# Token tiles 0 and 1 go through w_v unnormed, and their norm is applied afterwards

## Chip, cores and metric

The kernel runs on one core of a Trainium2 chip. The metric is the device time of one execution in microseconds. Before the change the median of three runs is 1320.01 us (1317.74 to 1320.96).

The engines are named as in the profile: PE is TensorE (matmuls and transposes), DVE is VectorE, ACT is ScalarE, POOL is GpSimd, SP is SyncE, which here only issues loads. Each has its own queue of instructions, and takes them in order.

## The reference, cut to what matters

The model is one layer: a mixing block (a gated convolution beside attention) and a feed-forward block, 1024 tokens by 1024 channels in 32-bit floats. Only its first step is touched here: the norm of the tokens and the projection to v and the forget logits.

```python
def rmsnorm(x, g):
    return x * lax.rsqrt(jnp.mean(x * x, axis=-1, keepdims=True) + 1e-6) * g

h = rmsnorm(x, norm_mix_pre)          # 1024 tokens x 1024 channels
proj = einsum("bsd,dn->bsn", h, w_in) # columns 1024:1544 are v (512) and 8 forget logits
logf = log_sigmoid(f_logit + b_f)
```

The factor of a token, rs = (mean(x*x) + 1e-6)^-0.5, is one number per row of h. It commutes with the projection: rs * ((x * g) @ w) is the same as (rs * x * g) @ w.

## The kernel before

The 1024 tokens are eight tiles of 128 rows. For each tile the kernel squares x with a sum along the row (ACT, output `ssq`), forms the factor on POOL (`rms_scale`: an addition `va`, then a power `r`), scales x to `hn`, and turns `hn` with eight 128x128 transposes on PE (`tp`) so that channels lie on the partitions. Each 32-bit operand is split in two halves, a high one (ACT copies, rounded) and a low one (DVE subtracts), and a product is the sum of three matmuls: high by high ("hh"), high by low ("hl"), low by high ("lh"). The tile's v and forget logits are `pv`: 8 channel blocks x 3 products x 2 column halves of 260, that is 48 matmuls a tile. `wvh` and `wvl` are the halves of w_v, block by block; `hB11h/hB11l` and `hB21h/hB21l` are the halves of the turned tiles 0 to 3 (channels 0 to 511 and 512 to 1023), and `hraw` is their unsplit copy, which later tiles subtract from. `vs` is pv copied out by ACT; POOL writes it to memory (`v_dram`), and DVE adds the bias `bf` to its last eight columns (`ff`).

Tiles 0 and 1 come while w_v is still being loaded, and are ordered by hand; the statements of that part are kept in program order on every engine (`strict[0] = engines`). Tile 0 is loaded in two halves and squared in two halves. Its factor comes first, then DVE scales one half and ACT the other, and only then do the transposes run (`t0.turn(hn)`). Since the gain g is per channel, it is put on after the transposes, by DVE (`scale`: hraw<-tp,gcol, where `gcol` is g turned by the small transpose `gps`); then ACT takes the high half (`high`) and DVE the low (`low`). Tile 1 goes the same way. In between, PE multiplies what is ready (`Parts.run`), and where nothing is, it multiplies zeros into a spare bank (`spins`, 512 columns each; 16 in all).

From tile 2 on, `norm` scales a whole tile in one DVE operation (hn<-xt,r,gm), two tiles ahead of its products: PE gets tile t+1's transposes, then tile t's 48 matmuls. There are three buffers for x, so the load of tile t+3 is issued only when tile t's buffer is free (`load_x` at the end of `norm_rest`). SP issues loads in the order of the statements.

After the eight tiles (`v_tile`), PE goes on with the products of the q, k and gate columns (`b`), for which the operands of all tiles are used.

Of the kernel before, what the change touches and what calls it, by code (L numbers as in the profile page):

```python
# [10 lines left out]
F32 = mybir.dt.float32  # L11
# [6 lines left out]
P = 128  # L18
# [28 lines left out]
def block_kernel(  # L47
# [114 lines left out]
    nc.vector.memset(ones, 1.0)  # L162
# [50 lines left out]
    av, av_close = pool("av")  # L213
    psa, psa_close = pool("psa", 4, space=PSUM)

    def load_x(st):
# [31 lines left out]
    nc.scalar.activation(warm, ones[:, 0:1], AF.Square)  # L248
    wvh = av.tile([P, KT, VF], F32R, name="wvh")
    wvl = av.tile([P, KT, VF], F32R, name="wvl")  # L250

# [4 lines left out]
        vs_tile()  # L256


    spin = psa.tile([P, 2, NC], F32, tag="pv", name="spin", bufs=2)
    zero = ap.tile([P, 4, P], F32R, tag="b12h", name="zero", bufs=2)  # L260
    nc.vector.memset(f32(zero), 0.0)
    sub(mask, tri, ident)
    nc.vector.tensor_scalar(mask, mask, BIG, None, op0=ALU.mult)

    def spins(n):
        for _ in range(n):
            nc.tensor.matmul(
                spin[:, 0, :], zero[:, 0, :], zero.rearrange("p a b -> p (a b)"),
                start=True, stop=True,
            )  # L270

    spins(7)
    gps = psa.tile([P, 4, P], F32, tag="mm", name="gps")[:, 0, :KT]
    nc.tensor.transpose(gps, g8, ident[:KT, :KT])
    nc.sync.dma_start(gm, norm_mix_pre[0].partition_broadcast(P))
    spins(3)

    def wv_high(k):
        copy(wvh[:, k, :], wrs[k])
# [3 lines left out]

    def norm_sum(st):

        xt = xq.popleft()
        hn = ap.tile([P, D], F32, tag="hn", name="hn", bufs=2)
        ssq = st_tile("ssq")
        nc.scalar.activation(hn, xt, AF.Square, scale=ROOT, accum_out=ssq)
        return xt, hn, ssq  # L290

    def norm_rest(st, xt, hn, rs):

        nc.vector.scalar_tensor_tensor(hn, xt, rs, gm, op0=ALU.mult, op1=ALU.mult)
        if st + 3 < ST:
            xq.append(load_x(st + 3))
# [6 lines left out]
    def turned(hn):  # L303

        tps = []
        for q in range(2):
            tp = psa.tile([P, 4, P], F32, tag="mm", name="tp")
            for k in range(4):
                kt = 4 * q + k
                nc.tensor.transpose(tp[:, k, :], hn[:, kt * P : (kt + 1) * P], ident)  # L310
            tps.append(tp)
        return tps

    hraw = av.tile([P, KT, NC], F32, name="hraw")

    class Scaled:


        def __init__(self, st):
            self.ss = slice(st * P, (st + 1) * P)  # L320
            self.ops = [tuple(t[:, :, self.ss] for t in b) for b in (hB11, hB21)]

        def raw(self, q):
            return hraw[:, 4 * q : 4 * q + 4, self.ss]

        def turn(self, hn):
            self.tps = turned(hn)

        def scale(self, q):
            g = gcol[:, 4 * q : 4 * q + 4].unsqueeze(2).broadcast_to([P, 4, P])  # L330
# [94 lines left out]
    xt = xq.popleft()
    hn = ap.tile([P, D], F32, tag="hn", name="hn", bufs=2)
    s2, part = st_tile("s2", 2), st_tile("nm")
    for n, c in enumerate((n1, n2)):
        nc.scalar.activation(
            hn[:, c], xt[:, c], AF.Square, scale=ROOT, accum_out=s2[:, n : n + 1]  # L430
        )
        if n == 0:
            nc.vector.tensor_scalar(part, s2[:, 0:1], EPS, None, op0=ALU.add)
    rs0 = rms_scale(s2[:, 1:2], part)
    nc.vector.tensor_scalar(hn[:, n1], xt[:, n1], rs0, None, op0=ALU.mult)
    nc.scalar.activation(hn[:, n2], xt[:, n2], AF.Identity, scale=rs0)
    nc.vector.tensor_copy(gcol, gps)
    xq.append(load_x(3))
    t0, t1 = Scaled(0), Scaled(1)
    t0.turn(hn)  # L440
    spins(4)
    xt1, hn1, ssq1 = norm_sum(1)
    wv_high(0)
    t0.scale(0)
    t0.high(0)

    def between():
        t0.scale(1)
        t0.low(0)

    rs1 = rms_scale(ssq1, between=between)
    v0, v1 = Parts(t0.ops), Parts(t1.ops)
    v0.run("hh", 0)
    spins(1)
    wv_high(1)
    v0.run("hh", 1)
    v0.run("lh", 0, 1)
    t0.high(1)
    nc.vector.tensor_scalar(hn1[:, n1], xt1[:, n1], rs1, None, op0=ALU.mult)
    nc.scalar.activation(hn1[:, n2], xt1[:, n2], AF.Identity, scale=rs1)  # L460
    xq.append(load_x(4))
    spins(1)
    t1.turn(hn1)
    wv_low(0)
    wv_high(2)
    v0.run("hh", 2)
    v0.run("lh", 2)
    v0.run("hl", 0)
    wv_high(3)
    t0.low(1)  # L470
    v0.run("hh", 3)
    v0.run("lh", 3)
    wv_high(4)
    t1.scale(0)
    t1.high(0)
    wv_low(1)
    v0.run("hh", 4)
    v0.run("lh", 4)
    v0.run("hl", 1)
    wv_high(5)  # L480
    t1.low(0)
    t1.scale(1)
    v1.run("hh", *range(4))
    v1.run("lh", *range(4))
    wv_high(6)
    wv_low(2)
    t1.high(1)
    v1.run("hl", 0, 1)
    t1.low(1)
    wv_high(7)  # L490
    wv_low(3)
    for k in (2,):
        v0.run("hl", k)
        v1.run("hl", k)
    v0.run("hh", 5)
    v0.run("lh", 5)
    xt2, hn, ssq2 = norm_sum(2)
    v0.run("hl", 3)
    v1.run("hl", 3)
    wv_low(4)  # L500
    v0.run("hh", 6)
    v0.run("lh", 6)
    sum3 = norm_sum(3)

    def between():
        for k in (5, 6, 7):
            wv_low(k)

    rs2 = rms_scale(ssq2, between=between)
    v1.run("hh", 4, 5)  # L510
    v1.run("lh", 4, 5)
    v0.run("hl", 4)
    v1.run("hl", 4)
    norm_rest(2, xt2, hn, rs2)
    v0.run("hh", 7)
    v0.run("lh", 7)
    v1.run("hh", 6)
    v1.run("lh", 6)
    v0.run("hl", 5, 6, 7)
    rs3 = rms_scale(sum3[2])  # L520
    v_out(0, v0.pv)
    v1.run("hh", 7)
    v1.run("lh", 7)
    v1.run("hl", 5, 6)
    cur = turn(2, hn)
# [1793 lines left out]
```

## Time and profile before

| what | before |
|---|---|
| median of three runs | 1320.01 us |
| lowest, highest | 1317.74, 1320.96 us |
| the profiled execution | 1319.89 us |
| its span in the trace | 1318.0 us |
| PE busy | 1308.8 us, 99% of the span |
| DVE, ACT, POOL busy | 917.2, 555.8, 185.6 us |
| PE's share of the chain that ended last | 96% |

The profiled execution is 1.89 us longer than its span. The page's chain of waits goes back from the last instruction to whatever released each step, so its shares say which engine set the end; the timeline views list one engine's instructions in order of start, and "idle before" there is the time the engine stood still ahead of an instruction, with what released it.

### The profile page before, as it was taken

To read this page: it belongs to the slowest core of one execution; us is meant where nothing else is said; L and a number is where in the kernel's file an instruction comes from. 1 tells how busy PE (TensorE), PEld (TensorE's weight loads), DVE (VectorE), ACT (ScalarE), POOL (GpSimd) and SP (SyncE) were. 2 spreads that over 40 slices of the span, in tenths; PEclk is the share of its full clock that TensorE was granted. 3 is DMA by queue.
4 is the path that set the end of the run, shared out by engine and by line. 5 is a ranking of instruction groups with operands and counts; after the bars stand their busy time and mean duration, and the time that the engine had idled before them with its cause. 6 is when DMAs were issued, how large, how long until landed. Compare 5 with 4: busy or idle time off the path is not lost.

```text
span 1318.0 us, 17686 instructions
## 1 busy us (share of the span) xinstructions
PE 1308.8 (99%) x6695; PEld 1089.3 (83%) x6695; DVE 917.2 (70%) x1313; ACT 555.8 (42%) x869; POOL 185.6 (14%) x347
## 2 busy tenths in 40 slices
PE   9999999999999999999999999999999999999998
PEld 8988888888888888888888888888888888888886
DVE  6883768776756866676667788866766666677674
ACT  6631323243355766513678432222322234344451
POOL 3101001012112212011223112111001110000001
PEclk9999999999999999999999999999999999999999
DMA  6352423556536445674476565533323337966551
GB/s 225 90 160 88 141 61 119 183 194 195 196 128 206 154 138 166 210 257 132 131 231 227 174 198 193 176 120 104 99 86 115 110 106 271 364 217 192 159 169 64
DMA packets 168389, 215.71 MB, mean 164 GB/s; under 512 B 11480, under 2 KB 113952, under 8 KB 168304
## 3 DMA queue, kind: packets, MB, share of 16 engines
q1 hardware_dynamic: 146352, 141.40, 34.5%
q0 software_dynamic: 21952, 73.19, 15.3%
q8 instruction: 52, 0.85, 0.3%
q14 instruction: 33, 0.27, 0.1%
HBM read 153.41 MB, written 61.15 MB: 163 GB/s over the span
## 4 chain that ended last, share of the span: by engine, by line
PE 96%; ACT 1%; DVE 1%; DMA 1%; issue 1%; POOL 0%; DVEq 0%; POOLq 0%; SPq 0%; ACTq 0%
PE b L76 61%; PE pd L76 16%; PE pv L76 4%; PE pbb L76 3%; PE pba L76 3%; PE po L76 2%; PE tps L76 2%; PE sp L76 2%; PE tp L76 1%; PE ma L76 1%; PE mb L76 1%; DMA raw<-in_w_gate_up_dram 0%; ACT raw L76 0%; DMA xt<-in_x_dram 0%; DVE x L76 0%
## 5 line engine op out<-in xcount | busy, mean ns | idle before, releaser
L76 DVE TENSOR_TENSOR c<-c,b 128x512 f32<-128x512 f32 x215 | 146.8, 683 | 96.9 <-PE b L76 87.4
L76 DVE TENSOR_TENSOR lo<-raw,hi 128x1024 fp32r<-128x1024 f32 (+1 forms) x91 | 109.7, 1205 | 81.2 <-PE b L76 65.7
L76 ACT ACTIVATE hi<-raw 128x1024 fp32r<-128x1024 f32 (+1 forms) x98 | 99.7, 1017 | 102.0 <-PE b L76 68.5
L76 ACT ACTIVATE hi<-sx 128x1024 fp32r<-128x1024 f32 x44 | 46.8, 1063 | 207.2 <-PE b L76 181.3
L76 DVE TENSOR_TENSOR lo<-sx,hi 128x1024 fp32r<-128x1024 f32 x44 | 53.8, 1223 | 39.6 <-PE b L76 37.9
L76 PE MATMUL b<-w12h,lo 128*128 128x512 f32 x208 | 80.9, 389 | 0.0
L76 PE MATMUL b<-w12h,hi 128*128 128x512 f32 x204 | 79.4, 389 | 0.0
L76 PE MATMUL b<-w12l,hi 128*128 128x512 f32 x204 | 79.4, 389 | 0.0
L76 PE MATMUL b<-hh,hi 128*128 128x512 f32 x176 | 69.0, 392 | 0.0
L76 PE MATMUL b<-hh,lo 128*128 128x512 f32 x176 | 68.5, 389 | 0.0
L76 PE MATMUL b<-hl,hi 128*128 128x512 f32 x176 | 68.5, 389 | 0.0
L76 DVE TENSOR_TENSOR sx<-raw 128x512 f32<-128x512 f32 x78 | 53.6, 687 | 20.0 <-DMA raw<-in_w_in_dram 10.3
L76 PE MATMUL b<-w,s4h 128*128 128x512 f32 x208 | 64.0, 389 | 0.0
L76 PE MATMUL pd<-hi,lo 128*128 128x512 f32 x160 | 62.3, 389 | 0.0
L76 PE MATMUL pd<-hi 128*128 128x512 f32 x160 | 61.9, 390 | 0.0
L76 PE MATMUL pd<-ghi 128*128 128x512 f32 x148 | 57.6, 389 | 0.0
L76 PE MATMUL pd<-ghi,glo 128*128 128x512 f32 x148 | 57.6, 389 | 0.0
L76 PE MATMUL pd<-glo,ghi 128*128 128x512 f32 x148 | 57.6, 389 | 0.0
L76 POOL DMA_DIRECT2D a_dramA<-um x33 | 17.9, 541 | 276.6 <-DVE um L76 275.8
L76 PE MATMUL b<-hT34h,hi 128*128 128x512 f32 x136 | 53.0, 390 | 0.4 <-DVE c L76 0.4
L76 PE MATMUL b<-hT34h,lo 128*128 128x512 f32 x136 | 52.9, 389 | 0.0
L76 PE MATMUL b<-hT12h,hi 128*128 128x512 f32 x136 | 52.9, 389 | 0.0
(451 smaller groups left out, 3572.8 us busy)
## 6 DMA issues: line engine op xcount, KB each, us to landing
raw<-in_w_gate_up_dram SPq DMA_DIRECT2D x52, 512.0 KB, 3.8
raw<-in_w_in_dram SPq DMA_DIRECT2D x35, 512.0 KB, 3.8
a_dramS<-um POOLq DMA_DIRECT2D x44, 256.0 KB, 3.1
a_dramA<-um POOLq DMA_DIRECT2D x33, 256.0 KB, 2.6
sg<-sg_dram SPq DMA_DIRECT2D x32, 256.0 KB, 4.2
graw<-a_dramS SPq DMA_DIRECT2D x14, 512.0 KB, 4.3
sg_dram<-c POOLq DMA_DIRECT2D x24, 256.0 KB, 2.5
raw<-in_w_down_dram SPq DMA_DIRECT2D x11, 512.0 KB, 4.4
```

What stands on the lines that cost most here:

```text
L76: ins = getattr(self.engine, name)(*args, **kw)
```

## The change

Tiles 0 and 1 are no longer scaled by their factor ahead of the transposes. PE turns x itself, half a tile at a time, and the products with w_v are those of x times g. The factor is put on at three later places: on v's rows, by the ACT copy out of pv (`v_out(..., scale=...rs)`); and on the columns of `hraw` that belong to tiles 0 and 1, by POOL, after a matmul of ones with the two factors on a diagonal (`rp`) has spread them over the partitions; `settle` then splits these columns anew into hB11 and hB21, where later products read them. Both tiles are loaded in halves, the first block of w_v between tile 0's halves. The squares of tiles 0 and 1 are whole tiles, in place in the x buffer; tile 1's now comes after those of tiles 2 and 3. The third x load, the row of gains `gm` and the fourth x load are issued later than before relative to w_v's blocks. The 32-byte bias row `bf`, broadcast to all partitions, is issued by POOL after tile 0's factor. The small load of gains for `gps` moves to ACT's queue. There are 4 spins of 512 columns and 10 of 256 in place of 16 of 512.

```diff
-        for c in (n1, n2) if st == 0 else (slice(0, D),):
+        for c in (n1, n2) if between else (slice(0, D),):
             nc.sync.dma_start(xt[:, c], rows[:, c])
+            if between and c is n1:
+                between()
...
-    xq = deque([load_x(0)])
-    nc.sync.dma_start(g8, norm_mix_pre[0].rearrange("(k p) -> k p", p=P))
-    xq.append(load_x(1))
-    for k in range(8):
+    nc.scalar.dma_start(g8, norm_mix_pre[0].rearrange("(k p) -> k p", p=P))
+    xts = [load_x(0, load_wv), load_x(1, lambda: None)]
+    for k in range(7):
         load_wv()
-        if k == 4:
-            xq.append(load_x(2))
+    xq = {2: load_x(2)}
...
+        def square(self):
+            self.ssq = st_tile("ssq")
+            nc.scalar.activation(
+                self.xt, self.xt, AF.Square, scale=ROOT, accum_out=self.ssq
+            )
...
+        nc.scalar.activation(
+            vs.rearrange("p (n c) -> p n c", n=2), pv[:, :, :hv], AF.Copy, **kw
+        )
...
+    def square(t):
+        if t < 2:
+            firsts[t].square()
+        else:
+            later[t] = norm_sum(t)
+        if t == 0:
+            nc.sync.dma_start(gm, norm_mix_pre[0].partition_broadcast(P))
+            xq[3] = load_x(3)
+        if t == 1:
+            xq[4] = load_x(4)
...
+    steps_(
+        "wh0 s00 wl0 x01 z1 h00 sq0 l00 phh00 phl00 z1 x10 s01 plh00 z1 pw0 x11 z2 s10 h01 wh1 l01 h10 "
...
+    hn = norm_rest(2, *later[2][:2], norms[2])
+    steps_("plh06 pw3 phh16 plh16 phl05 phl15 phh07")
+    hn3 = norm_rest(3, *later[3][:2], norms[3])
+    steps_("pw1")
+    cur = turn(2, hn)
+    hn = hn3
+    steps_("plh07 phl06 phl07")
+    v_out(0, parts[0].pv, scale=firsts[0].rs)
+    steps_("phh17 plh17 phl16 phl17")
+    v_out(1, parts[1].pv, scale=firsts[1].rs)
...
+    for t, f in enumerate(firsts):
+        nc.gpsimd.tensor_scalar(dg[:, t, :], ident, f.rs, None, op0=ALU.mult)
+    rp = psa.tile([P, 4, P], F32, tag="mm", name="rp")[:, :2, :]
+    nc.tensor.matmul(flat_(rp), ones, flat_(dg), start=True, stop=True)
+    copy(rb, flat_(rp))
...
+    for q in range(2):
+        nc.gpsimd.tensor_tensor(
+            raw_both(q), raw_both(q), rb.unsqueeze(1).broadcast_to([P, 4, 2 * P]),
+            op=ALU.mult,
         )
...
+        for q, (hh, hl) in enumerate((hB11, hB21)):
+            split(hh[:, :, both], hl[:, :, both], raw_both(q))
...
             v_out(2, v2.pv)
+            settle()
```

The order of the instructions on PE, at the start of the program, before (`spin` are the zeros, `tp` the transposes):

```order
L76 MATMUL spin<-zero 128x512 x7
L76 MATMUL gps<-ident,gm 128x8
L76 MATMUL spin<-zero 128x512 x3
L76 MATMUL tp<-ident,hn 128x128 x8
L76 MATMUL spin<-zero 128x512 x4
L76 MATMUL pv<-wvh,hB11h 128x260 x2
L76 MATMUL spin<-zero 128x512
L76 MATMUL pv<-wvh,hB11h 128x260 x2
L76 MATMUL pv<-wvh,hB11l 128x260 x4
L76 MATMUL spin<-zero 128x512
L76 MATMUL tp<-ident,hn 128x128 x8
```

And now:

```order
L76 MATMUL spin<-zero 128x512 x4
L76 MATMUL tp<-ident,xt 128x128 x4
L76 MATMUL gps<-ident,gm 128x8
L76 MATMUL spin<-zero 128x256 x4
L76 MATMUL tp<-ident,xt 128x128 x4
L76 MATMUL spin<-zero 128x256
L76 MATMUL pv<-wvh,hB11h 128x260 x2
L76 MATMUL pv<-wvl,hB11h 128x260 x2
L76 MATMUL spin<-zero 128x256
L76 MATMUL tp<-ident,xt 128x128 x4
L76 MATMUL pv<-wvh,hB11l 128x260 x2
L76 MATMUL spin<-zero 128x256
```

The transposes of tile 0 read `xt` in place of `hn`, come in fours, and follow 4 spins where they followed 10.

On PE, later, where tile 2's products begin and tile 3's transposes follow, before:

```order
L76 MATMUL pv<-wvh,hB11h 128x260 x8
L76 MATMUL pv<-wvl,hB11h 128x260 x8
L76 MATMUL pv<-wvh,hB11l 128x260 x6
L76 MATMUL tp<-ident,hn 128x128 x8
L76 MATMUL pv<-wvh,hB11l 128x260 x2
```

And now:

```order
L76 MATMUL pv<-wvh,hB11h 128x260 x8
L76 MATMUL pv<-wvl,hB11h 128x260 x8
L76 MATMUL pv<-wvh,hB11l 128x260 x6
L76 MATMUL rp<-rs,ones 128x256
L76 MATMUL tp<-ident,hn 128x128 x8
L76 MATMUL pv<-wvh,hB11l 128x260 x2
```

The matmul with ones stands between 22 of tile 2's products and tile 3's transposes.

On POOL, from tile 1's factor on (`v_dram` the write of v, `rs<-ident` the diagonals, `hraw<-hraw,rs` the multiplication of the columns), one piece of the difference:

```order
-L76 TENSOR_SCALAR va<-ssq 128x1
-L76 TENSOR_TENSOR r_481<-va,power 128x1
-L76 TENSOR_SCALAR va<-ssq 128x1
-L76 TENSOR_TENSOR r_562<-va,power 128x1
+L76 TENSOR_SCALAR rs<-ident,r_277 128x128
+L76 TENSOR_SCALAR rs<-ident,r_412 128x128
+L76 TENSOR_TENSOR hraw<-hraw,rs 128x4x256 x2
+L76 TENSOR_SCALAR va<-ssq 128x1
+L76 TENSOR_TENSOR r_564<-va,power 128x1
 L76 DMA v_dram<-vs 128x512
```

Between the factor of tile 4 (which now stands ahead of the second write of v) and that of tile 5 there are now two diagonals and two multiplications. On ACT the square of tile 5 stands behind the two copies that read their results (`hB11h<-hraw` and `hB21h<-hraw`, 128x4x256), and the square of tile 4 stands ahead of tile 1's `vs`:

```order
L76 ACTIVATE vs<-pv,r_277 128x520
L76 ACTIVATE hn,ssq<-xt 128x1024
L76 ACTIVATE vs<-pv,r_412 128x520
L76 ACTIVATE rs<-rp 128x256
L76 ACTIVATE hraw<-tp 128x4x128 x2
L76 ACTIVATE hB11h<-tp 128x4x128
L76 ACTIVATE hB21h<-tp 128x4x128
L76 ACTIVATE hB11h<-hraw 128x4x256
L76 ACTIVATE hB21h<-hraw 128x4x256
L76 ACTIVATE hn,ssq<-xt 128x1024
```

## Rows read from the trace of the kernel before

**Rows 1.** Page: busy time by engine, and the chain's shares.

```profile
PE 1308.8 (99%) x6695; PEld 1089.3 (83%) x6695; DVE 917.2 (70%) x1313; ACT 555.8 (42%) x869; POOL 185.6 (14%) x347
...
PE 96%; ACT 1%; DVE 1%; DMA 1%; issue 1%; POOL 0%; DVEq 0%; POOLq 0%; SPq 0%; ACTq 0%
```

**Rows 2.** Chain of waits, first 30 us: start us, us, engine, operation.

```profile
1.17 3.29 DMA xt<-in_x_dram
...
6.82 1.97 PE tp L76 x8
8.79 1.71 PE spin L76 x4
10.50 0.43 PE pv L76 x2
...
12.17 0.87 PE tp L76 x8
13.04 10.31 PE pv L76 x86
...
24.48 2.91 PE pv L76 x22
```

**Rows 3.** Chain of waits from 24 to 64 us: tile 5's transposes.

```profile
38.01 0.87 PE tp L76 x8
```

**Rows 4.** Two stretches: us, busy us by engine, PEclk, DMA share, GB/s.

```profile
5.00:10.00 5.00, 4.90 (x16) 3.77 (x17) 2.43 (x5) 3.85 (x9) 1.64 (x4) 1.00 0.95 338
25.00:60.00 35.00, 35.00 (x298) 35.00 (x298) 31.18 (x46) 23.59 (x39) 6.12 (x13) 1.00 0.28 88
```

**Rows 5.** Timeline of ACT: start us, us, engine, line, operation, out<-in.

```profile
24.80 0.61 ACT L76 ACTIVATE vs<-pv 128x520 f32<-128x520 f32 x1
...
25.76 1.09 ACT L76 ACTIVATE hn<-xt 128x1024 f32<-128x1024 f32 x1
26.71 0.22 ACT L76 ACTIVATION_READ_ACCUMULATOR hn<-xt 128x1 f32 x1
```

**Rows 6.** Timeline of DVE, same columns.

```profile
8.83 0.69 DVE L76 TENSOR_TENSOR hraw<-tp,gcol 128x512 f32<-128x512 f32 x1 [0.16 <-PE tp L76]
9.44 0.68 DVE L76 TENSOR_TENSOR hB11l<-hraw,hB11h 128x512 fp32r<-128x512 f32 x1
...
19.69 1.28 DVE L76 SCALAR_TENSOR_TENSOR hn<-xt,r,gm 128x1024 f32<-128x1024 f32 x1
...
65.29 1.22 DVE L76 TENSOR_TENSOR lo<-raw,hi 128x1024 fp32r<-128x1024 f32 x1 [0.78 <-ACT hi L76]
```

**Rows 7.** Timeline of POOL, same columns.

```profile
18.10 0.87 POOL L76 TENSOR_TENSOR r<-va,power 128x1 f32<-128x1 f32 x1
...
25.71 0.54 POOL L76 DMA_DIRECT2D v_dram<-vs  x1 [1.01 <-ACT vs L76]
27.02 0.22 POOL L76 TENSOR_SCALAR va<-ssq 128x1 f32<-128x1 f32 x1 [0.77 <-DVE hn L76]
27.33 0.57 POOL L76 TENSOR_TENSOR r<-va,power 128x1 f32<-128x1 f32 x1
```

**Rows 8.** POOL, groups by shape: count, busy us, mean ns, idle before.

```profile
L76 POOL TENSOR_TENSOR rows<-rows,mask 128x128 f32<-128x128 f32 x32 | 14.5, 457 | 62.2 <-DVE nm L76 56.3 <-DMA rows<-c_dram 5.8
```

**Rows 9.** Timeline around 441 us: a POOL row, the DVE row beside it.

```profile
440.82 0.90 POOL L76 TENSOR_TENSOR yb<-cb,mask 128x128 f32<-128x128 f32 x1
...
440.62 1.65 DVE L76 TENSOR_TENSOR yl<-raw,yh 128x512 fp32r<-128x512 f32 x2
```

**Rows 10.** DMA issues, 20.9 to 25 us: count, KB, us to landing.

```profile
xt<-in_x_dram SPq DMA_DIRECT2D x1, 512.0 KB, 3.5
```

**Rows 11.** The same for the first 30 us.

```profile
xt<-in_x_dram SPq DMA_DIRECT2D x7, 512.0 KB, 4.3
```

**Rows 12.** PE, the plain 32-bit matmuls with ones: min/median/max ns.

```profile
L76 PE MATMUL cps<-s,ones x2: 275/275/275, 134.4 to 134.5; 128*128 128x64 f32 x2
```

**Rows 13.** Timeline of PE: the first matmul with the next weights' low half.

```profile
69.82 0.39 PE L76 MATMUL b<-hB11h,lo 128*128 128x512 f32 x1
```

More of the change, by code (lines that the diff above doesn't have):

```diff
@@ L214, in block_kernel, with load_x @@
     psa, psa_close = pool("psa", 4, space=PSUM)
-    def load_x(st):
+    def load_x(st, between=None):
         xt = ax.tile([P, D], F32, tag="x", name="xt", bufs=3)
         rows = x2d[st * P : (st + 1) * P, :]
-        for c in (n1, n2) if st == 0 else (slice(0, D),):
+        for c in (n1, n2) if between else (slice(0, D),):
             nc.sync.dma_start(xt[:, c], rows[:, c])
+            if between and c is n1:
+                between()
         return xt
@@ L237, in block_kernel @@
     strict[0] = engines
+    zero = ap.tile([P, 4, P], F32R, tag="b12h", name="zero", bufs=2)
+    nc.vector.memset(f32(zero), 0.0)
+    nc.vector.memset(ones, 1.0)
     gm = ax.tile([P, D], F32, name="gm")
     g8 = gm[:KT, :P]
-    xq = deque([load_x(0)])
-    nc.sync.dma_start(g8, norm_mix_pre[0].rearrange("(k p) -> k p", p=P))
-    xq.append(load_x(1))
-    for k in range(8):
+    nc.scalar.dma_start(g8, norm_mix_pre[0].rearrange("(k p) -> k p", p=P))
+    xts = [load_x(0, load_wv), load_x(1, lambda: None)]
+    for k in range(7):
         load_wv()
-        if k == 4:
-            xq.append(load_x(2))
+    xq = {2: load_x(2)}
     warm = st_tile("warm")
-    nc.scalar.activation(warm, ones[:, 0:1], AF.Square)
+    nc.scalar.activation(warm, f32(zero)[:, 0, 0:1], AF.Square)
     wvh = av.tile([P, KT, VF], F32R, name="wvh")
@@ L256, in block_kernel, with flat_, spins @@
         vs_tile()
-    spin = psa.tile([P, 2, NC], F32, tag="pv", name="spin", bufs=2)
-    zero = ap.tile([P, 4, P], F32R, tag="b12h", name="zero", bufs=2)
-    nc.vector.memset(f32(zero), 0.0)
+    def flat_(t):
+        return t.rearrange("p a b -> p (a b)")
+    spin = psa.tile([P, 4, P], F32, tag="mm", name="spin")
+    spin = flat_(spin)
     sub(mask, tri, ident)
     nc.vector.tensor_scalar(mask, mask, BIG, None, op0=ALU.mult)
-    def spins(n):
+    def spins(n, w=4):
         for _ in range(n):
             nc.tensor.matmul(
-                spin[:, 0, :], zero[:, 0, :], zero.rearrange("p a b -> p (a b)"),
+                spin[:, : w * P], zero[:, 0, :], flat_(zero[:, :w, :]),
                 start=True, stop=True,
             )
-    spins(7)
+    spins(4)
     gps = psa.tile([P, 4, P], F32, tag="mm", name="gps")[:, 0, :KT]
-    nc.tensor.transpose(gps, g8, ident[:KT, :KT])
-    nc.sync.dma_start(gm, norm_mix_pre[0].partition_broadcast(P))
-    spins(3)
     def wv_high(k):
@@ L301, in norm, with turned @@
         return norm_rest(st, xt, hn, rms_scale(ssq))
[L303 to L312, printed above, removed]
+    def turned(hn, q):
+        tp = psa.tile([P, 4, P], F32, tag="mm", name="tp")
+        for k in range(4):
+            kt = 4 * q + k
+            nc.tensor.transpose(tp[:, k, :], hn[:, kt * P : (kt + 1) * P], ident)
+        return tp
     hraw = av.tile([P, KT, NC], F32, name="hraw")
-    class Scaled:
+    class First:
         def __init__(self, st):
@@ L321, in __init__, with turn @@
             self.ops = [tuple(t[:, :, self.ss] for t in b) for b in (hB11, hB21)]
+            self.tps, self.xt = {}, xts[st]
         def raw(self, q):
             return hraw[:, 4 * q : 4 * q + 4, self.ss]
-        def turn(self, hn):
-            self.tps = turned(hn)
+        def turn(self, q):
+            self.tps[q] = turned(self.xt, q)
         def scale(self, q):
@@ L337, in low, with root @@
             sub(self.ops[q][1], self.raw(q), f32(self.ops[q][0]))
+        def square(self):
[3 more added lines that the diff above has]
+            )
+        def root(self):
+            self.rs = rms_scale(self.ssq)
     def turn(st, hn):
         ss = slice(st % 4 * P, (st % 4 + 1) * P)
-        tps = turned(hn)
+        tps = [turned(hn, q) for q in range(2)]
         if st < 4:
@@ L412, in block_kernel, with v_out @@
     flast = []
-    def v_out(st, pv):
+    def v_out(st, pv, **kw):
         vs = vs_tile()
-        copy(vs.rearrange("p (n c) -> p n c", n=2), pv[:, :, :hv])
+        nc.scalar.activation(
+            vs.rearrange("p (n c) -> p n c", n=2), pv[:, :, :hv], AF.Copy, **kw
+        )
         nc.gpsimd.dma_start(v_dram[st * P : (st + 1) * P, :], vs[:, :AW])
@@ L422, in v_out @@
             flast.clear()
[L425 to L430, printed above, removed]
-        )
[L432 to L525, printed above, removed]
@@ L526, in block_kernel, with root @@
-    v1.run("hl", 7)
+    firsts = [First(t) for t in range(2)]
+    later, norms = {}, {}
+    def square(t):
[8 more added lines that the diff above has]
+            xq[4] = load_x(4)
+    def root(t):
+        if t < 2:
+            firsts[t].root()
+            if t == 0:
+                nc.gpsimd.dma_start(bf, b_f[0].partition_broadcast(P))
+        else:
+            norms[t] = rms_scale(later[t][2])
@@ new lines, in step, with steps_ @@
+    def step(o):
+        n = int(o[-1])
+        if o[0] == "z":
+            return spins(n, 2)
+        if o[:2] in ("wh", "wl", "sq", "pw"):
+            return dict(wh=wv_high, wl=wv_low, sq=square, pw=root)[o[:2]](n)
+        if o[0] == "x":
+            return firsts[int(o[1])].turn(n)
+        if o[0] == "p":
+            return parts[int(o[3])].run(o[1:3], n)
+        getattr(firsts[int(o[1])], dict(s="scale", h="high", l="low")[o[0]])(n)
+    def steps_(row):
+        for o in row.split():
+            step(o)
@@ new lines, in block_kernel @@
+    firsts[0].turn(0)
+    nc.tensor.transpose(gps, g8, ident[:KT, :KT])
+    spins(4, 2)
+    nc.vector.tensor_copy(gcol, gps)
+    parts = [Parts(f.ops) for f in firsts]
+    steps_(
[5 rows of a table added]
+    )
+    hn = norm_rest(2, *later[2][:2], norms[2])
[7 more added lines that the diff above has]
+    steps_("phh17 plh17 phl16 phl17")
@@ new lines, in block_kernel, with raw_both @@
+    v_out(1, parts[1].pv, scale=firsts[1].rs)
+    z = z_tile("rs")
+    dg = z[:, : 2 * P].rearrange("p (t c) -> p t c", t=2)
+    rb = z[:, 2 * P : 4 * P]
+    for t, f in enumerate(firsts):
[3 more added lines that the diff above has]
+    copy(rb, flat_(rp))
+    both = slice(0, 2 * P)
+    def raw_both(q):
+        return hraw[:, 4 * q : 4 * q + 4, both]
```

11 lines of the change are left out of this document (4 added, 7 removed), and 4 rows, old and new, of the table parts.

## The prediction, made before the changed kernel ran

> **What bounds the kernel now.** First the page: PE is busy 99% of the span and makes 96% of the chain that ended last [rows 1]. So the end moves only by what moves PE's work, and the place to look is the one stretch that the change touches, the first 60 us. The chain of waits there [rows 2] leaves the loads and the norm of tile 0 at 6.82 us, when PE starts tile 0's transposes, and from then on stays on PE, whatever the other engines do. What counts is therefore where tile 2's first product stands (24.48 us before) and whether PE then keeps going: the products of tiles 2 to 7 that follow are the same in both kernels.
>
> In these first microseconds PE runs at two speeds. Eight transposes take 1.97 us from 6.82 on and 0.87 us from 12.17 on; two matmuls of pv take 0.43 us at 10.50, and 86 of them 10.31 us later, 0.120 each [rows 2]. So the first rows run at 1.2 GHz and the later at 2.4, and the step lies at about 10.9 us, after PE had been busy, mostly with spins, for some 9 us. The granted clock reads 1.00 for that stretch [rows 4], so it is the rows that tell the level, not that column.
>
> **What the early start is worth.** Before, PE does, ahead of 10.9 us, eight transposes and two products of pv that count, the rest is spins. From there at full speed: tile 1's eight transposes 0.87, 94 products at 0.120 = 11.28, tile 2's transposes 0.87, two spins of 0.23 = 0.46: 13.5, which gives 24.4 against 24.48 in the row.
>
> Now the transposes read x itself. The factor of tile 0, between the landing of its second half at 1.17 + 3.29 = 4.46 and 6.82 [rows 2], is off the path. Against that a block of w_v, 260 KB, is loaded ahead of the second half; at the 338 GB/s of that stretch [rows 4] it costs 0.8 to 1.2 us, so the second four transposes start at 5.3 to 5.7. From 5.5, in the new order and at half speed (0.215 each): 12 transposes, six products and spins as wide as one product bring PE to 10.4; to 10.9 two or three more products. Ahead of the step stand now 16 transposes and about 8.5 products. Left: 87.5 x 0.120 = 10.5, two short spins 0.23, tile 2's transposes 0.87: tile 2 starts at 10.9 + 11.6 = 22.5. **Gain 1.95 us.** Bounds: if x lands 1.2 late, some five instructions (0.55 us) less; if the clock steps up 2.4 us sooner, as PE's work starts no later than before, half of that more, 1.2. If gaps in PE's new start delay the step, less by half the delay.
>
> **The wait that takes its place.** In front of tile 3's transposes PE now meets `rp`, the matmul that spreads the factors. It waits for POOL's two diagonals, and POOL takes its queue in order: tile 4's `va` and `r`, tile 1's write of v, then the diagonals. So `rp` waits for tile 4's square, that for tile 4's load, and that for the buffer which tile 2's scaling on DVE gives back. Priced row by row: the scaling started at 19.69 and takes 1.28 [rows 6]. DVE's queue ahead of it loses two half-tile scalings and holds as before 16 operations 0.61 apart (8.83, 9.44); I let it move with PE, by 1.95, so that it ends at 19.0. The one load that ran alone took 3.5 us [rows 10]: 22.5. The square with its read takes 1.17 [rows 5]: 23.7. `va` and `r` together, 27.02 to 27.90 [rows 7]: 24.6. The write's issue, 0.54 [rows 7]: 25.1. The diagonals, 128x128 with one operand, are not in the trace; they lie between 0.22 (one column [rows 7]) and 0.46 (two operands [rows 8]), I take 0.33 each: 25.8 to 25.9.
>
> PE comes to `rp` at 22.5 + 2.9 [rows 2] = 25.4. **Wait 0.5**, and 0.3 more for the halting of POOL beside DVE that the next paragraph shows: 0.8, bounds 0 and 1.9 (the load at the median of 4.3 [rows 11] and both haltings). `rp` itself, 256 columns of plain 32-bit, has two bounds: 0.12 as 260 columns of pv, and four times the 0.275 of 64 columns [rows 12], 1.1; I take 0.4, nearer the first, since 0.275 is mostly the length of one pass. Then tile 3's second four transposes need a bank that ACT gives back with its copy of `rp`: 256 columns, under the 0.61 of 520 [rows 5], against four transposes of 0.43 that hide it: 0.25 visible, bounds 0 and 0.6.
>
> POOL is held up when DVE reads two operands from SBUF. At 18.10 a power of one column took 0.87 beside DVE's subtractions of weights, at 27.33, beside an operation with one operand in PSUM, 0.57 [rows 7]; the 128x128 mask, 0.457 in the mean of 32 [rows 8], took 0.90 beside DVE's yl<-raw,yh, which itself took 1.65 for two [rows 9] where two of DVE's 512-column steps are 0.61 apart [rows 6]. So both lose some 0.3 to 0.45 us a meeting. The Trainium skill, "SBUF — State Buffer", section "Who interferes with whom" and the points on the two sides ahead of it, says that the second of two such instructions is blocked until the first is through; the rows of 441 us agree in sign, and by that rule a long multiplication of POOL would hold DVE for its whole length.
>
> **The columns of tiles 0 and 1.** POOL multiplies 128x1024 twice. No row has that shape. From one column (0.22) to 128 (0.457) the step is 0.24, and eight of them with the start are 2.15; upper bound eight whole instructions, 3.66; I take 2.2, since the fixed part is paid once. The Trainium skill, "GPSIMD Engine Reference", section 3.1, gives 2.6 cycles an element for tensor_tensor, an estimate of 2.2 us; by it the sum is the same. What is queued behind: ACT's two high copies wait for the results, and behind them stands tile 5's square; on POOL tile 5's factor. After `rp` at 26.2 and its copy: 26.9, multiplications to 29.1 and 31.3, ACT's copy 1.09 [rows 5], tile 5's square 1.17, `va` and `r` 0.9, the scaling 1.28: 35.8. PE needs it for tile 5's transposes, at 38.01 [rows 3] less what is gained, 37.5. It is covered with 1.7 us to spare; the cost is nothing as long as that lasts.
>
> DVE gets two subtractions of 1024, 1.22 each [rows 6], 2.4 in all, between 25 and 60 us, where it is idle 35.0 - 31.2 = 3.8 [rows 4]; what is pushed past that has the slack at the next stage, where the weights' low half is done at 66.5 [rows 6] and first read at 69.82 [rows 13]. No cost. ACT (23.6 of 35 busy) carries the copies and the whole squares. The load of `gps` on ACT's queue, the bias row issued early on POOL and the scale on v's copy are beside other work: nothing.
>
> **Sum.** -1.95 + 0.8 + 0.4 + 0.25 = -0.5 us. On the profiled execution, 1319.89 (span 1318.0 and 1.89 around it), that is **1319.4**; the median of the three runs lies 0.12 above that execution, which I leave aside. A measurement of this kernel tells about 0.3%, 4.0 us, from no change; so this is no change. What makes the estimate stiff: whatever PE gains or loses ahead of 25 us is largely taken up at `rp`, whose time hangs on a load and not on PE.
>
> **Rivals.**
> 1. *The chain to `rp` is quicker.* If DVE's scaling of tile 2 comes 1 us sooner, PE meets no wait there: -1.95 + 0.4 + 0.25 = -1.3, 1318.6; with the earlier step of the clock too -2.5, 1317.4. For it: DVE's queue starts some 3 us earlier. Against: the weights, which it also follows, land at the rate of before [rows 4]. Even with both it is short of 4.0.
> 2. *POOL's multiplication is slow, and PE waits at tile 5's transposes: slower than before.* At 3.66 each the multiplications end at 34.2, and the chain behind them at 38.7, with a halting beside DVE 39.2: PE, due at 37.5, stands 1.2 to 1.7 us. 1319.4 + 1.5 = 1320.9. It decides from about 3.05 each on, where the 1.7 to spare are used. For it: no row of that size, and the haltings [rows 9]. If DVE is held for a whole multiplication, its subtraction for the first settled half is late by up to 2.2, the spare is gone, and the time is the same 1320 to 1321. This is what the rule of the Trainium skill named above would bring here.
> 3. *The load of tile 4 is late.* At 4.3 us in place of 3.5 and with POOL halted twice, `rp` waits 1.9: 1320.5. With rival 2 together 1322.
> 4. *The change doesn't start PE sooner*, because the halves of x are behind the w_v block: the transposes start at 6.7, tile 2 at 23.1. `rp` still comes at 25.9, PE at 26.0: -1.4 + 0.1 + 0.65, the same 1319.3.
>
> **Chances.** The forecast with rival 4, 1318.8 to 1320.2: 0.50. Rival 1: 0.20, of which half for a gain that no row shows and that goes past 4.0 (a start-up at full clock and no wait). Rivals 2 and 3: 0.30, of which 0.09 for sums beyond 4.0. Faster by over 0.3%: 0.10; within 0.3%: 0.81; slower by over 0.3%: 0.09. The range that leaves out a tenth on each side is 1317.0 to 1322.0.
>
> **What would show it.** In the trace of the changed kernel tile 2's first pv<-wvh,hB11h should start at 22.5 (21.3 to 23.2); `rp` should have idle time of PE ahead of it, 0.5 to 1.5 us, released by POOL, and start near 26; POOL's hraw<-hraw,rs should be near 2.2 us, and tile 5's transposes start without idle time. The step of the spacing from 0.215 to 0.120 shows the clock. I am wrong if `rp` starts without a wait (then rival 1), if hraw<-hraw,rs is over 3 us (rival 2), or if PE's time changes after 60 us, which nothing here foresees.

## The result, and the profile after

The changed kernel takes 1321.42 us in the median of 20 runs (1318.88 to 1322.73), the kernel before 1319.39 in the median of 20 (1317.74 to 1320.96). The ratio is 1.0014, with a 95% interval of 1.0008 to 1.0021: it is slower by 1.1 to 2.8 us. That is small, but clear of the noise. The prediction had 1319.4 and a small gain; the time lies inside its range, the sign is the other one.

The profiled execution took 1321.18 us with a span of 1319.3, so 1.3 us more span than the one of before. The whole 1.3 us is there by the time PE reaches tile 4's transposes, at 32.66 where they were at 31.39. The chain of waits (start, duration, what) of the kernel before, where tile 3's and tile 4's transposes stand:

```profile
27.39 0.87 PE tp L76 x8
28.27 3.12 PE pv L76 x26
31.39 0.87 PE tp L76 x8
```

And that of the changed kernel from 24 us on:

```profile
24.50 1.77 POOL rs L76 x2
...
26.32 0.70 PE rp L76 x2
27.02 1.65 PE tp L76 x8
28.67 4.00 PE pv L76 x26
32.66 0.87 PE tp L76 x8
...
39.29 0.87 PE tp L76 x8
```

And PE's timeline of that stretch, with the idle time ahead of an instruction in brackets:

```profile
20.99 1.22 PE L76 MATMUL pv<-wvh,hB11h 128*128 128x260 f32 x8
...
26.32 0.70 PE L76 MATMUL rp<-rs,ones 128*128 128x256 f32 x2 [2.43 <-POOL rs L76]
...
28.90 1.84 PE L76 MATMUL pv<-wvh,hB21h 128*128 128x260 f32 x8
30.58 1.12 PE L76 MATMUL pv<-wvl,hB21h 128*128 128x260 f32 x8
...
32.50 1.04 PE L76 MATMUL tp<-ident,hn 128*128 128x128 f32 x8
```

Tile 2's first product starts at 20.99 and not at 24.48 [rows 2]: 3.49 us sooner. Then PE stands 2.43 us ahead of `rp`, released by POOL's diagonals (`rs`). `rp` takes 0.70. Tile 3's eight transposes take 1.65 where they took 0.87, and the 26 products behind them 4.00 where they took 3.12. The sum is -3.49 + 2.43 + 0.70 + 0.78 + 0.88 = +1.30, which is the whole difference of the spans: tile 5's transposes come at 39.29, 1.28 after 38.01 [rows 3], and the difference of the spans is the same, so on balance nothing is gained or lost from there to the end.

The last two terms are the surprise. Eight products of 260 columns take 1.84 us at 28.90 and 1.12 at 30.58. Three stretches of the same trace (columns as in [rows 4], PEclk after the busy times) say why:

```profile
24.00:26.00 2.00, 0.00 (x0) 0.00 (x0) 1.44 (x2) 0.00 (x0) 1.95 (x3) 1.00 0.69 277
26.00:31.00 5.00, 4.68 (x24) 4.31 (x25) 1.29 (x2) 3.35 (x6) 3.68 (x3) 0.66 0.39 105
31.00:36.00 5.00, 5.00 (x45) 5.00 (x45) 4.09 (x3) 3.71 (x8) 2.69 (x4) 1.00 0.01 3
```

PE does nothing from 24 to 26 us, and in the five microseconds after that its granted clock is 0.66, a stretch partly at 1.2 GHz, before it is back at 1.00.

The chain that made `rp` late, on POOL, then ACT, then DVE:

```profile
23.00 0.22 POOL L76 TENSOR_SCALAR va<-ssq 128x1 f32<-128x1 f32 x1 [1.12 <-ACT hn L76]
23.30 0.57 POOL L76 TENSOR_TENSOR r<-va,power 128x1 f32<-128x1 f32 x1
23.83 0.62 POOL L76 DMA_DIRECT2D v_dram<-vs  x1
24.50 1.76 POOL L76 TENSOR_SCALAR rs<-ident,r 128x128 f32<-128x128 f32 x2
27.58 4.73 POOL L76 TENSOR_TENSOR hraw<-hraw,rs 128x1024 f32<-128x1024 f32 x2 [1.32 <-ACT rs L76]
```

```profile
21.75 1.06 ACT L76 ACTIVATE hn<-xt 128x1024 f32<-128x1024 f32 x1 [0.81 <-DMA xt<-in_x_dram]
```

```profile
16.79 1.28 DVE L76 SCALAR_TENSOR_TENSOR hn<-xt,r,gm 128x1024 f32<-128x1024 f32 x1 [0.77 <-POOL r L76]
...
23.90 1.28 DVE L76 SCALAR_TENSOR_TENSOR hn<-xt,r,gm 128x1024 f32<-128x1024 f32 x1 [2.52 <-POOL r L76]
...
31.09 2.31 DVE L76 TENSOR_TENSOR hB11l<-hraw,hB11h 128x1024 fp32r<-128x1024 f32 x1 [0.80 <-ACT hB11h L76]
33.43 1.23 DVE L76 TENSOR_TENSOR hB21l<-hraw,hB21h 128x1024 fp32r<-128x1024 f32 x1
```

Tile 2's scaling on DVE ends at 18.07, tile 4's load is issued at once and squared from 21.75, its factor is ready at 23.87, the write of v is issued, and then the two diagonals take 1.76 us: 1.17 for the first, beside DVE's scaling of tile 4 (23.90 to 25.18), and 0.59 for the second. The two multiplications take 4.73, 2.4 each.

### The profile page after: what moved, and what is told of

Read it like the earlier page. It is cut to its first block, busy times and chain, and to the rows that moved or that the text cites. A ratio compares the mean times of both kernels' runs of the same rounds, so it can differ in the third digit from the quotient of the medians.

```text
span 1319.3 us, 17686 instructions
## 1 busy us (share of the span) xinstructions
PE 1307.6 (99%) x6695; PEld 1089.6 (83%) x6695; DVE 920.1 (70%) x1312; ACT 557.1 (42%) x868; POOL 192.9 (15%) x351
## 4 chain that ended last, share of the span: by engine, by line
PE 96%; DVE 2%; ACT 1%; issue 1%; DMA 0%; POOL 0%; DVEq 0%; POOLq 0%; ACTq 0%
PE b L76 60%; PE pd L76 16%; PE pba L76 3%; PE pbb L76 3%; PE pv L76 3%; PE po L76 2%; PE tps L76 2%; PE sp L76 2%; PE tp L76 1%; PE ma L76 1%; PE mb L76 1%; DMA raw<-in_w_gate_up_dram 0%; DVE um L76 0%; DVE c L76 0%; PE spin L76 0%
## 5 line engine op out<-in xcount | busy, mean ns | idle before, releaser
L76 PE MATMUL b<-hT34l,hi 128*128 128x512 f32 x136 | 53.0, 390 | 0.0
```

Source lines behind the costliest of these rows:

```text
L76: ins = getattr(self.engine, name)(*args, **kw)
```

## The experiments

The two kernels' traces are single executions, and the start of an execution varies by about a microsecond, so each experiment is read by its median against the kernel before on the same chip, and by its trace.

**e1: fill the wait.** 21 matmuls of zeros between tile 2's 22 products and `rp`. (The 22 products were also written out ahead of `rp`, so that PE's order stays that of the changed kernel. The same was done in e2, e9, e4, e5 and e6, whose edits are shown in pieces.)

```diff
-    rp = psa.tile([P, 4, P], F32, tag="mm", name="rp")[:, :2, :]
+    rp = psa.tile([P, 4, P], F32, tag="mm", name="rp")
+    for _ in range(21):
+        nc.tensor.matmul(
+            flat_(rp)[:, 2 * P :], zero[:, 0, :], flat_(zero[:, :2, :]),
+            start=True, stop=True,
+        )
+    rp = rp[:, :2, :]
```

> The changed kernel with 21 matmuls of zeros (128x256) between tile 2's 22 products and rp, where PE stood idle for 2.43 us; nothing else moves. Theory A (the idle time lets PE's clock fall, and the half-speed stretch after it costs as much as the wait): rp still starts near 26.3 us, since POOL sets it, but PE's rows after it are at full speed (eight transposes 0.87 and not 1.65 us, products 0.12 apart), rp takes 0.35 and not 0.70, and the time falls by about 2.0 us, from 1321.4 to 1319.4. Theory B (PE's slow rows after rp are waits for banks or for ACT's copies): the rows keep their spacing and the time stays at 1321.4.

Measured: 1320.55 us, ratio to before 1.0009 (1.0000 to 1.0018). PE's timeline:

```profile
24.68 2.67 PE L76 MATMUL rp<-zero 128*128 128x256 f32 x21
27.45 0.70 PE L76 MATMUL rp<-rs,ones 128*128 128x256 f32 x2
27.99 1.35 PE L76 MATMUL tp<-ident,hn 128*128 128x128 f32 x8
...
29.43 1.11 PE L76 MATMUL pv<-wvh,hB21h 128*128 128x260 f32 x8
...
32.29 1.04 PE L76 MATMUL tp<-ident,hn 128*128 128x128 f32 x8
```

The eight products behind `rp` take 1.11 us and not 1.84, at the same place in the program, and the granted clock from 26 to 31 us is 1.00 and not 0.66. From `rp` to tile 4's transposes it is 27.45 to 32.29, 4.84 us; in the changed kernel 26.32 to 32.50, 6.18. So theory A holds for the cause: the idle time costs a second time, by a slower clock after it. The size was set too high, at 2.0; it is 1.3 to 1.6 (see the table below), since `rp` takes its 0.70 at either clock and half of the transposes' delay stays. It is the trace that shows this and not the median: by the ratios e1 is 0.7 us under the changed kernel, and the two intervals overlap. `rp` itself came 1.1 us later in this execution, because loads of x landed later: PE waits 1.03 us for tile 0's second half, whose transposes start at 7.03 and not at 5.71, and ACT's square of tile 2 waits for its load until 15.61, where it started at 14.25. That moves everything behind it.

**e2: the diagonals early.** The same two instructions of POOL, moved from behind tile 4's factor and the write of v to right behind tile 1's factor.

```diff
     steps_("pw1")
+    z = z_tile("rs")
+    dg = z[:, : 2 * P].rearrange("p (t c) -> p t c", t=2)
+    rb = z[:, 2 * P : 4 * P]
+    for t, f in enumerate(firsts):
+        nc.gpsimd.tensor_scalar(dg[:, t, :], ident, f.rs, None, op0=ALU.mult)
     cur = turn(2, hn)
```

> The changed kernel with POOL's two diagonals moved ahead of the first write of v and of tile 4's factor, right behind tile 1's factor; PE's order is the same. Theory A (rp waits for what stands ahead of the diagonals in POOL's queue): the diagonals are done by 22.5 us, rp starts without a wait at 23.7, PE's clock stays up, tile 4's transposes start at 31.4 - 3.5 + 0.35 + 0.25 = 28.5 in place of 32.7, and the time is 1321.4 - 4.1 = 1317.3 (2.1 below before). Rival (the diagonals are slow or late wherever they stand, since DVE halts POOL): rp still waits over 1 us, and the time is 1319 or more.

Measured: 1318.15 us, ratio 0.9992 (0.9983 to 1.0001), 2.9 us under the changed kernel by the ratios, where 4.1 was expected. PE's timeline, and POOL's and DVE's beside it:

```profile
23.81 0.88 PE L76 MATMUL pv<-wvh,hB11l 128*128 128x260 f32 x6
24.52 0.60 PE L76 MATMUL rp<-rs,ones 128*128 128x256 f32 x2
24.96 1.35 PE L76 MATMUL tp<-ident,hn 128*128 128x128 f32 x8
```

```profile
21.61 1.23 POOL L76 TENSOR_SCALAR rs<-ident,r 128x128 f32<-128x128 f32 x2
...
25.69 5.03 POOL L76 TENSOR_TENSOR hraw<-hraw,rs 128x1024 f32<-128x1024 f32 x2 [0.29 <-ACT rs L76]
```

```profile
26.03 2.37 DVE L76 TENSOR_TENSOR ff<-vs,bf 128x8 f32<-128x8 f32 x1
```

`rp` starts without idle time, and the clock holds. The theory is right: it was POOL's queue. The diagonals take 0.63 each here, where DVE's only neighbour with two operands in SBUF is an eight-column addition; in the changed kernel the one beside DVE's scaling took 1.17 and the one after it 0.59.

**e3: without the columns.** POOL's multiplications and the new splits left out; the columns of tiles 0 and 1 stay unnormed.

```diff
-    for q in range(2):
-        nc.gpsimd.tensor_tensor(
-            raw_both(q), raw_both(q), rb.unsqueeze(1).broadcast_to([P, 4, 2 * P]),
-            op=ALU.mult,
-        )
...
-            settle()
```

> The changed kernel without POOL's two multiplications of hraw and without the new splits of tiles 0 and 1's columns (two copies on ACT, two subtractions on DVE): the columns stay unnormed. Theory A (this work lies beside PE's and costs nothing): 1321.4 within 0.7, tile 5's transposes at 39.3 us as in the changed kernel. Rival (the multiplications hold DVE and ACT up, which is where the 2 us went): 1319.4 or less.

Measured: 1321.69 us, ratio 1.0021 (1.0012 to 1.0030): as the changed kernel or worse. This work costs nothing while PE comes late, as predicted. PE waited 2.66 us for the diagonals, and its rows behind `rp` were slow again:

```profile
27.23 0.70 PE L76 MATMUL rp<-rs,ones 128*128 128x256 f32 x2 [2.66 <-POOL rs L76]
27.77 1.81 PE L76 MATMUL tp<-ident,hn 128*128 128x128 f32 x8
```

**b1: the kernel before with short spins.**

```diff
-        for _ in range(n):
+        for _ in range(2 * n):
             nc.tensor.matmul(
-                spin[:, 0, :], zero[:, 0, :], zero.rearrange("p a b -> p (a b)"),
+                spin[:, 0, : 2 * P], zero[:, 0, :],
+                zero[:, :2, :].rearrange("p a b -> p (a b)"),
                 start=True, stop=True,
```

> The kernel before with each matmul of zeros of 512 columns replaced by two of 256, nothing else. In the changed kernel the clock rose at 7.1 us after 5.7 us of PE's work, in the kernel before at 10.9 after 9.3. Theory A (the shorter matmuls with their more frequent weight loads are what lets it rise sooner): here too it rises 2 us or more before 10.9, and the time falls by 1 us or more, to 1318.4. Theory B (it is the transposes of data, or chance of the execution): it rises at 10.9 within 1 us, or at another time without a pattern, and the time is 1319.4 within 0.7.

Measured: 1319.36 us, ratio 1.0001 (0.9992 to 1.0010). The clock rose at about 5.2 us in this trace, and it brought little: tile 2's first product stands at 24.05, 0.43 before the first trace's 24.48, and the median is that of the kernel before.

```profile
5.04 0.98 PE L76 MATMUL spin<-zero 128*128 128x256 f32 x6
6.48 1.10 PE L76 MATMUL tp<-ident,hn 128*128 128x128 f32 x8 [0.45 <-DVE hn L76]
...
9.98 0.51 PE L76 MATMUL pv<-wvh,hB11h 128*128 128x260 f32 x2 [1.46 <-ACT hB11h L76]
```

The transposes take 1.10 and not 1.97 us [rows 2], and then PE stands 1.46 us until ACT has made the high half. That is a limit which the prediction had not seen in the kernel before. Behind these 1.46 us the rows are at full speed: the clock did not fall.

**b2: the kernel before, a second trace.** No edit.

> The kernel before once more, as it is, for a second trace of its start. Theory A (the step of PE's clock at 10.9 us is this kernel's own): it lies within 1 us of 10.9. Theory B (it is chance): it lies elsewhere, and tile 2's first product is still at 24 to 24.5 us, since the first product waits for ACT's high half and not for the clock.

One run, 1318.55 us:

```profile
6.45 1.03 PE L76 MATMUL tp<-ident,hn 128*128 128x128 f32 x8
...
9.25 0.51 PE L76 MATMUL pv<-wvh,hB11h 128*128 128x260 f32 x2 [0.85 <-ACT hB11h L76]
```

The unchanged kernel's clock had risen by 6.45 us this time, where the first trace has it at 10.9. Theory B holds in its first half: when the clock rises differs from execution to execution, and short spins can't be made out as its cause. Its second half failed: tile 2's first product stands at 23.34, outside the 24 to 24.5 that were expected and 1.1 sooner than in the first trace.

**a2: the changed kernel, a second trace.** No edit.

> The changed kernel once more, as it is, for a second trace. Theory A (the loads of x and the step of PE's clock fall at other times in each execution, and rp's time follows the loads): the step lies anywhere from 5.5 to 8 us, rp starts at 26.3 to 27.5 after an idle time of 2 to 3 us, eight transposes behind it take 1.8 us again, and the time is 1321.4 within 0.7. Theory B (the trace of the changed kernel was one odd execution): the idle time ahead of rp is under 1 us.

Measured: 1321.18 us, ratio 1.0018 (1.0009 to 1.0027).

```profile
26.78 0.70 PE L76 MATMUL rp<-rs,ones 128*128 128x256 f32 x2 [2.42 <-POOL rs L76]
27.31 1.71 PE L76 MATMUL tp<-ident,hn 128*128 128x128 f32 x8
28.67 0.78 PE L76 MATMUL pv<-wvh,hB11l 128*128 128x260 f32 x2
29.25 1.94 PE L76 MATMUL pv<-wvh,hB21h 128*128 128x260 f32 x8
```

2.42 us of idle time again, and the slow rows behind it. The first trace was no odd one. Here the clock rose about a microsecond later, PE was through with tile 2's 22 products 0.47 us later, and `rp` came 0.46 later: `rp` moved with PE, and the wait stayed as it was.

**e5: without rp.** Diagonals, `rp`, its copy, multiplications and splits left out; the columns stay unnormed.

> The changed kernel without rp, its diagonals, its copy, POOL's multiplications and the new splits: the columns of tiles 0 and 1 stay unnormed, so it shows what the early start alone is worth. Theory A (the whole loss lies at rp): tile 3's transposes follow 2.7 us after tile 2's first product without idle time, and the end is 3 to 3.5 us before that of the kernel before in the trace: 1316.5, 4.9 less than the changed kernel. Rival (the early start itself brings little, since later steps take it back): 1319 or more.

Measured: 1317.80 us, ratio 0.9994 (0.9985 to 1.0003). That is neither theory's time. In the trace the first b product stands at 59.89, where it stands at 63.46 in the first trace of before and at 62.30 in the second. But 1.6 us of that is lost again far behind:

```profile
PE b L76 <- DVE c L76: 1.3, 2, 0.9
PE tp L76 <- ACT raw L76: 0.7, 1, 0.7
```

These waits, of 0.7 near 697 us and of 0.9 near 782 for the larger ones, are also in the second trace of the changed kernel (0.7 and 0.7) and in part, from 0.4 to 0.9, in its first and in those of b1, e4, e6, e9 and the second of e2, and in neither trace of before nor in those of e1, e3 and the first of e2; the same kernel has them in one execution and not in another. That the median shows about 1 us where the traces' starts differ by 2.4 to 3.6 is not fully explained by that, and stays open.

**e9: the diagonals on ACT.** At their place in the program, but as ACT's copies.

```diff
-        nc.gpsimd.tensor_scalar(dg[:, t, :], ident, f.rs, None, op0=ALU.mult)
+        nc.scalar.activation(dg[:, t, :], ident, AF.Copy, scale=f.rs)
```

> The changed kernel with the two diagonals made by ACT (a copy of the identity scaled by the factor) right behind tile 1's v, instead of by POOL behind tile 4's factor and the write of v; PE's order is the same. In the changed kernel the last link ahead of rp was 0.62 us of POOL's issue and 1.77 us of diagonals beside DVE's scaling of tile 4. Theory A (these two links make the wait): ACT is through with v at 23.5, the diagonals with 0.3 each at 24.1, rp starts at 24.2 to 25 with 0.3 to 1 us of idle time, the eight transposes behind it take 1.1 us and not 1.8, and the time is 1321.4 - 3 = 1318.4. Rival (the load of tile 4 makes the wait, and the diagonals come late on any engine): rp at 26 or later, over 1320.5.

Measured: 1318.17 us, ratio 0.9993 (0.9984 to 1.0002). The trace is of the longest of the eleven runs, 1321.27 us, with the clock's rise at 10.5 and tile 2's first product only at 22.82:

```profile
25.99 0.70 PE L76 MATMUL rp<-rs,ones 128*128 128x256 f32 x2 [0.27 <-ACT rs L76]
26.53 1.29 PE L76 MATMUL tp<-ident,hn 128*128 128x128 f32 x8
...
27.90 1.11 PE L76 MATMUL pv<-wvh,hB21h 128*128 128x260 f32 x8
```

0.27 us of idle time, no slow rows behind. `rp` at 25.99 is by itself no evidence against the rival, which had 26 or later, since the whole start is late here; counted from tile 2's first product it comes after 3.17 us, in the changed kernel after 5.33. With that, and with a time 2.8 us below the changed kernel's by the ratios, theory A holds: POOL's last two links made the wait.

**e4 and e6: what comes next.** e4 is e2 with ACT's unsplit copies of tile 2 placed ahead; e6 also calls for the new splits after tile 3's products.

```diff
     v_out(0, parts[0].pv, scale=firsts[0].rs)
+    cur[1]()
...
-            settle()
...
             rest()
+            if st == 3:
+                settle()
```

> The kernel with the early diagonals (e2), and ACT's two unsplit copies of tile 2 (hraw<-tp) moved from behind the copy of rp to behind tile 0's v. Theory A (tile 3's second four transposes wait for a bank that these copies give back, not for the copy of rp itself): the eight transposes take 0.87 us and not 1.11, 0.25 us less than e2, 1317.9. Rival (they wait for the copy of rp): as e2, 1318.1. Tile 4's square comes about 1.5 us later by this; if that is too late for its transposes, it is slower than e2.

> The kernel e4 (early diagonals, unsplit copies first), with the new splits of tiles 0 and 1's columns called for after tile 3's products instead of after tile 2's, so that ACT's square of tile 5 stands ahead of them. In e4 PE stood 0.8 us at tile 4's products, for halves that ACT and DVE made late, behind these splits. Theory A (the splits, waiting for POOL's multiplications, hold ACT's queue, and that is the next limit): no idle time of PE at tile 4's products, the first b product 60.5 us in place of 62.3, and the time 1.5 to 2 us under e4's, 1317.5. Rival (DVE's total work up to 60 us is the limit): the idle time moves to a later tile and the time stays at 1319.

e4: 1319.38 us, ratio 1.0002 (0.9993 to 1.0010). Its transposes behind `rp` take 1.04 in one row instead of 1.35, so they did wait for the bank; but the time is about 1 us above e2's, though the intervals overlap. PE stood 0.8 us:

```profile
PE pv L76 <- DVE b12l L76: 0.5, 1, 0.5
PE pv L76 <- ACT b12h L76: 0.3, 1, 0.3
```

The expectation of e6 put that at tile 4's products; in PE's timeline it is at 49.8 and 50.7, tile 6's. DVE is busy 14.24 of the 15 us from 45 to 60; that its low half came late behind other subtractions, whose order moved with the edit, is argued and not tested. So e6 was aimed at the wrong place: 1318.84, ratio 0.9997 (0.9988 to 1.0006), 0.3 of idle time left at tile 7's. It does not decide between its theories.

**e2 again.** No edit to e2.

> The kernel with the early diagonals (e2) once more, for a tighter interval. Its trace had the first b product at 61.5 us, against 63.5 and 62.3 in the two traces of the kernel before: 1.4 us less, so 1317.9 against 1319.3, a ratio of 0.9989. Rival (the first result was chance): a ratio of 1.000 or more.

Measured: 1318.49 us, ratio 0.9996 (0.9987 to 1.0005). e2 is faster than the changed kernel: both its intervals end below 1.0008. Against the kernel before it is 0.5 to 1 us ahead in both sets, which can't be told from no change. No version tried is clearly faster than before.

The traces side by side, all read from PE's timelines, in us:

| kernel | clock full from | idle ahead of rp | rp | rp to tile 4's transposes | first b |
|---|---|---|---|---|---|
| before | 10.9 | | | | 63.46 |
| before again | 6.5 | | | | 62.30 |
| b1, before with short spins | 5.2 | | | | 63.02 |
| changed | 6.7 | 2.43 | 26.32 | 6.18 | 64.75 |
| changed again | 7.8 | 2.42 | 26.78 | 6.38 | 65.40 |
| e3, no columns | 8.0 | 2.66 | 27.23 | 6.36 | 65.82 |
| e1, filled | by 7.0 | 0 | 27.45 | 4.84 | 64.53 |
| e9, on ACT | 10.5 | 0.27 | 25.99 | 4.77 | 63.01 |
| e2, early | 8.1 | 0 | 24.52 | 4.73 | 61.50 |
| e2 again | 7.5 | 0 | 24.14 | 4.73 | 61.11 |
| e4, copies first | 6.8 | 0 | 23.84 | 4.41 | 62.29 |
| e6, late splits | 10.5 | 0 | 25.41 | 4.41 | 62.85 |
| e5, no rp | 6.4 | | | | 59.89 |

The expectation of b1 has the changed kernel's rise at 7.1; by the spacing of its products it is 6.7. The fifth column falls into two groups, 6.2 to 6.4 behind a wait of over 2.4 us and 4.7 to 4.8 without one: 1.3 to 1.6 us for the clock. (In e4 and e6 it is 4.4, since the wait for the bank is gone as well.) The mean of the first b product is 65.3 in the three traces with the wait and 62.9 in the two of before: 2.4 later, against 2.0 by the medians.

## Why the prediction was wrong, point by point

**What bounds the kernel** was right: what PE loses in the first 33 us is, between the two profiled executions, in the span to a tenth.

**The steps that failed** are two terms of the sum, both at `rp`: the wait, put at 0.8 with an upper bound of 1.9, is 2.4 to 2.7; and what PE's clock does behind such a wait, for which the sum has no term at all, is 1.3 to 1.6.

**The early start** was put at 1.95 us. Between the two profiled executions it is 3.49, between the second traces of both kernels 1.88, and 2.5 between the means of the two traces of before (23.9) and of the three with the changed start and the wait (21.4). So its size was about right, and it isn't what turned the sign. What does not hold is the fixed time of the clock's rise, "the step lies at about 10.9 us": it was one execution's. Over all traces it lies from 5.2 (b1) to 10.9 us (the first trace of before), and twice at over 10 with the changed kernel's start (e9, e6). The start itself was read rightly: the second four transposes at 5.71, predicted 5.3 to 5.7.

**The wait at rp** was named at the right place. That `rp` came at 26.32, with 25.8 to 26.2 predicted, is luck, for two errors meet in it: PE's start was 1.5 us earlier than predicted, and the chain to `rp` 2.0 longer. Counted from tile 2's first product, `rp` was predicted 3.3 us later, 3.6 with one halting, and comes 5.33, 5.32 and 5.55 later in the three traces with the wait. Of the 2.0 us beyond 3.3, 1.1 are the diagonals: 1.76 in place of 0.66. The row taken as their upper bound, 0.46 for a mask with two operands, was too low even without a neighbour (0.59 for the second one), and beside DVE's scaling the first takes 1.17. 0.6 are DVE's scaling of tile 2, which ends 2.9 us ahead of tile 2's first product where 3.5 were assumed: it didn't move with PE by all of PE's gain. 0.2 are the load, 3.68 from the end of that scaling to the square, predicted 3.5. The rest is in small links. And the claim that makes the estimate stiff, that `rp` hangs on a load and takes up what PE gains or loses, isn't borne out: in the three traces with the wait PE's start differs by 0.7, `rp` follows it, and the wait stays at 2.4 to 2.7.

**What was left out**: PE's clock falls when PE stands still for 2.4 us, and the sum counted a wait at its own length. That is 1.3 to 1.6 us. Between the two profiled executions the prediction's own sum is -3.49 + 2.43 + 0.70 + 0.25 + 1.4 = +1.3; without the last term it would be -0.1. By the means of the traces (start, wait, `rp` with the bank, clock) it is -2.5 + 2.5 + 0.9 + 1.5 = +2.4, as the first b product has it.

**A row that was misread** changed little: at 27.33 POOL's power of 0.57 does not stand beside an operation with one operand in PSUM but beside two eight-column additions with both operands in SBUF, 0.26 us in all.

**rp, its copy and the bank** were put at 0.65; `rp` takes 0.44 to the next instruction in e2, and the transposes behind it 0.3 longer than in the kernel before: right in size. But the bank is given back by the unsplit copies on ACT, as e4 shows, and not by the copy of `rp`.

**The columns** cost nothing (e3), and POOL's multiplications took 2.4 each, predicted 2.2. Rival 2 did not happen in the changed kernel. But the rule of the Trainium skill, "SBUF — State Buffer", "Who interferes with whom", weighed there (of a VectorE instruction with two operands in SBUF and a GpSimd instruction that reads SBUF, the second is blocked until the first is through), agrees with the rows: DVE's subtraction of 1024 columns takes 2.31 us at 31.09 beside a multiplication and 1.23 behind it; in e2 an addition of eight columns takes 2.37, until the first multiplication is through. It was counted as 0.3 to 0.45 a meeting; here it is up to 2.2, nearly the whole length of POOL's instruction. It costs no time here because PE is not waiting for those halves.

**Rival 1** (no wait at all) was priced at 1318.6; e2 and e9, which remove the wait, took 1318.2 to 1318.5.

## What to carry to other kernels

Price a wait of TensorE by its length and by what the clock does behind it; a gain that ends in a wait can be turned into a loss. Before moving work to the queue of an engine off the critical path, ask what stands ahead of it there: two small instructions moved up in POOL's queue undid the whole loss. And do not build a sum on the time of an event, such as the clock's rise, that has been seen in one execution.

## What the runs showed of the hardware

- Behind 2.4 us without work PE's rows ran at half speed from 26.3 to about 30.6, with a granted clock of 0.66 from 26 to 31; behind 0.27 us (e9) and behind 1.46 us (b1, at 9.98) they did not. At the start the clock reads 1.00 [rows 4] while the rows of that time are at half speed [rows 2].
- The rise at the start came at 5.2 to 10.9 us in traces of the same few kernels, at 6.5 and 10.9 for the same program, though PE's work began at 1.4 to 1.6 in all. What decides it is open.
- `rp`, 256 columns of plain 32-bit, appears as two rows. To the next instruction it takes 0.53 us with the clock low (26.32 to 26.85), 0.54 in e1 and e9 with the clock at 1.00, and 0.44 in e2, where no wait stands ahead of it: these rows do not show a difference by the clock.
- One eight-column addition of DVE took 2.37 us beside a multiplication of POOL (e2), 0.16 at 21.23 in the changed kernel.
